# Four chunks of B and C in the state-space part, projected with tokens on partitions and turned by transposing transfers

## The chip, the cores and the metric

The kernel runs on one core of a Trainium2 chip, as one program. The time is device microseconds of one execution; below the median of the runs is given with their lowest and highest. Times inside an execution are microseconds from the start of its span, as the hardware profiler recorded them.

## What is computed

Two transformer blocks run one after the other on x of 256 tokens x 2048 features, in fp32: block 0 mixes with differential attention, block 1 with a state-space model (Mamba-2 style), and each is followed by a gated feed-forward network. The change lies in block 1's mixer:

```python
proj = h @ w_in                      # 256 x 2048 times 2048 x 10304
z, xbc, dt = jnp.split(proj, [4096, 4096 + 6144], axis=-1)
xbc = silu(causal_conv4(xbc, conv_w) + conv_b)       # along the tokens, each column for itself
xs, bm, cm = jnp.split(xbc, [4096, 4096 + 1024], axis=-1)
...
cb = jnp.einsum('btgn,bsgn->btsg', cc, bc)           # state products, 8 groups
y_intra = jnp.einsum('btsg,btsgh,bsghp->btghp', cb, decay, xdt)
...
return rms_norm((y + d_skip * xs) * silu(z)) @ w_out
```

B (bm) and C (cm) are columns 8192 to 10239 of the projection, x is columns 4096 to 8191, z columns 0 to 4095, and the last 64 columns are the step sizes dt. The convolution runs over time with four taps, so the kernel wants it with features on partitions and tokens along the free dimension, where a tap is a shifted slice.

## The kernel before, in words

Every weight matrix is streamed from DRAM in units of 256 rows x up to 512 columns. For a unit SyncE issues the load (`split_unit`, L261, a ring of 7 buffers named raw), ScalarE casts it to the rounded type fp32r (wh, L264), VectorE computes the remainder (wl = raw - wh), and TensorE makes three products per tile of 128 rows: wh with the high and the low part of the activations (ah, al), and wl with the high part. wh and wl have rings of 4 buffers: the cast of a unit waits until TensorE has ended the unit four before it. The remainder is put into VectorE's program one step late (`low_parts`, `lagging`), behind whatever the step before it issued there. Line 126 in the profile is a helper through which all of TensorE's and VectorE's instructions go, so tiles tell them apart: mm, wk and po are PSUM banks, bc holds B and C, xc the x columns of one group.

There are two ways to multiply a unit. `products` (through `push_k4`) makes the 128 tokens of a half the stationary operand and the weights the moving one: n columns per matmul, 2 x 2 x 3 matmuls per unit, tokens on partitions in the result. `feature_products` (through `push_features`) makes 128 weight columns stationary and the 256 tokens moving: n/128 x 2 x 3 matmuls of 256 columns per unit, features on partitions in the result.

The order of the work is written by generators. Each unit popped from the queue is one tick (`tick`), which steps every active generator once; a `yield` is a wait of one tick. The order of a chunk's follow-up work is thus fixed against the units of the chunks behind it, on all engines. Each of ScalarE, VectorE, TensorE and SyncE takes its instructions in that order. Beside the units run "ada" jobs (`dot_job`): SyncE loads 512 KB of the modulation matrix into the same ring raw (L498), and VectorE multiplies and sums it; in the stretch of B and C two per chunk.

Block 1 goes through its columns in the order 9856 (448 columns: 3 tiles of C and dt), 8192 (512), 8704, 9088, 9472 (384 each), then x0, z0, x1, z1, ... x7, z7 (512 each). All are eight units long.

- Chunk 9856 has tokens on partitions and is turned by TensorE (`conv_tokens`).
- Chunks 8192 to 9472 have features on partitions (`push_features`), and `conv_features` convolves them straight out of PSUM (`conv_tile`: one ScalarE instruction for the last tap and the bias, three VectorE instructions for the others), one tile of 128 features per tick, then a silu on ScalarE. x7 is done in the same way.
- Chunks x0 to x6 have tokens on partitions and go through `conv_turned` (L1856): ScalarE copies the two PSUM banks into the room of xc as 16-bit halves, all low halves ahead of all high ones; two ticks later SyncE issues two transposing transfers of 16-bit elements (L1864) into a room that is free by then (`y_turned`); three ticks later ScalarE puts the halves of two tiles together into the tile xin (L1870) and the convolution runs on that.

When the last chunk of B and C is convolved, `state_products` multiplies B with C for the eight groups, two groups per tick, and then loads the decay data of group 0 from DRAM by GpSimd's queue (`load_decay`, 1 MB). `y_steps` of group 0 uses that after z0.

Of the kernel before, what the change touches and what calls it, by code (L numbers as in the profile page):

```python
# [15 lines left out]
U16 = mybir.dt.uint16  # L16
# [80 lines left out]
def block_kernel(ctx: ExitStack, tc: tile.TileContext, x, x_t, columns_in, ssd_columns, da_columns, c, ada_w,  # L97
# [53 lines left out]
    def tmp(name="tmp"):  # L151
        return t2.tile([128, 512], F32, tag="t2", name=name)
# [1702 lines left out]

    def conv_turned(banks, xc, g):  # L1856
        hs = [xc[:, 2 * b:2 * b + 2, :].rearrange("p k t -> p (k t)").bitcast(U16) for b in range(2)]
        for b in range(2):
            act.copy(hs[b].rearrange("p (e f) -> p e f", e=2), banks[b].bitcast(U16).rearrange("p (f e) -> p e f", e=2))
        xT = [half_tiles(y_turned(g + 1)[:, b]) for b in range(2)]  # L1860
        for _ in range(2):
            yield
        for b in range(2):
            sp.dma_start_transpose(xT[b], hs[b])  # L1864
        for _ in range(3):
            yield
        for p in range(2):
            xin = tmp("xin").rearrange("p (k t) -> p k t", k=2)
            for b in range(2):
                act.copy(xin[:, :, b * 128:(b + 1) * 128].bitcast(U16).rearrange("p k (t e) -> p k t e", e=2),  # L1870
                         xT[b].rearrange("p (e k) t -> p k t e", e=2)[:, 2 * p:2 * p + 2])
            for i in range(2):
                conv_tile(xin[:, i, :], xc[:, 2 * p + i, :], 4 * g + 2 * p + i)
                yield
        act.activation(xc, xc, AF.Silu)
        yield

    def x_steps(g, banks):
        gp, h0 = S["gp"], 8 * g
        xc = gp.tile([128, 4, 256], F32, tag="xc", name="xc")  # L1880
        if g < TURNED:
            yield from conv_turned(banks, xc, g)
        else:
            yield from conv_features(banks, 4, xc, 4 * g)
# [126 lines left out]
    for col, n in ((9856, 448), (8192, 512), (8704, 384), (9088, 384), (9472, 384)):  # L2011
        bk = Banks()
        if n == 448:
            cross(end, norm, wi, col, n, bk, enter)
        else:
            norm.push(wi, col, n, bk, True)

        def take_bc(bk=bk, n=n, col=col):
            nt = 3 if n == 448 else n // 128
            t0 = (col - 8192) // 128  # L2020
            gens = [(conv_tokens if n == 448 else conv_features)(bk(), nt, S["bc"][:, t0:t0 + nt, :], 32 + t0)]
            if n == 448:
                gens.append(step_sizes(bk()))
            if col == 9472:
                last = gens[0]

                def then():
                    yield from last
                    yield from state_products()
                gens = [then()]  # L2030
# [131 lines left out]
```

## Time and profile before

| what | us |
|---|---|
| median of 3 runs (lowest to highest) | 2579.22 (2576.81 to 2579.29) |
| the profiled execution, its own time | 2578.1 |
| its span, first to last instruction | 2576.4 |
| TensorE busy in the span | 2551.2 (99%) |
| VectorE busy | 2110.8 (82%) |
| ScalarE busy | 1507.5 (59%) |
| stretch of chunks 8192 to 9472 (1213.34 to 1289.73), VectorE busy in it | 76.39, 62.88 |
| ScalarE busy in that stretch | 43.52 |

The page gives an engine's busy time and share of the span, then the chain of work that ended last by engine and line. A row of a timeline has start, duration, engine, line, operation, the tiles written and read, the shape, how many instructions were merged, and in brackets how long the engine had been idle and what ended the wait. A duration of a TensorE instruction reaches to the end of its pipeline, so the spacing of starts is its cost. A row of the stretches has the window, then the busy time of TensorE, its weight loads, VectorE, ScalarE and GpSimd with the number of instructions, the granted clock, the share of the DMA engines and GB/s. The clock was granted in full (0.999 on average).

### The profile page before, as it was taken

How to read it: one execution, taken by the hardware profiler on the slowest of the kernel's cores; microseconds unless marked ns; L12 is line 12 of the kernel's file. 1: busy time of each engine (PE TensorE's matmuls, PEld its weight loads, DVE VectorE, ACT ScalarE, POOL GpSimd, SP SyncE). 2: the span in 40 equal slices, each digit the busy share in tenths (PEclk: the TensorE clock that was granted, in tenths of full speed). 3: DMA queues.
4: the chain of work that ended last, by engine and by line, in shares of the span. 5: the costliest groups of instructions: out<-in, count | busy, mean ns of one | idle time of the engine just before them, and what ended most of it. 6: DMA issues, size and time to landing. Idle time of an engine off the chain costs nothing.

```text
span 2576.4 us, 34370 instructions
## 1 busy us (share of the span) xinstructions
PE 2551.2 (99%) x12144; PEld 2092.2 (81%) x12144; DVE 2110.8 (82%) x2955; ACT 1507.5 (59%) x2059; POOL 145.4 (6%) x225
## 2 busy tenths in 40 slices
PE   8999999999999999999999999999999999999999
PEld 5667778888888888888988888888888888888887
DVE  6779988778988898777878788888779999897675
ACT  4446654555655564446557777686566666665443
POOL 0014431000000000000000100000000000000000
PEclk9999999999999999999999999999999999999999
DMA  9987888699999869994677988878756667678884
GB/s 388 398 313 285 278 293 318 257 316 321 339 332 371 294 223 344 340 345 131 210 268 249 301 249 274 278 233 270 248 169 210 210 221 209 215 219 269 290 286 170
DMA packets 272989, 704.42 MB, mean 273 GB/s; under 512 B 101408, under 2 KB 109856, under 8 KB 271536
## 3 DMA queue, kind: packets, MB, share of 16 engines
q1 hardware_dynamic: 250960, 683.49, 76.8%
q10 hardware_dynamic: 17760, 4.43, 1.5%
q0 software_dynamic: 4096, 14.29, 1.5%
q8 instruction: 95, 1.56, 0.2%
q14 instruction: 78, 0.64, 0.1%
HBM read 680.53 MB, written 2.20 MB: 265 GB/s over the span
## 4 chain that ended last, share of the span: by engine, by line
PE 90%; DVE 4%; ACT 2%; DMA 2%; issue 1%; ACTq 0%; SPq 0%; POOL 0%; DVEq 0%; POOLq 0%
PE mm L126 62%; PE wk L126 22%; PE po L126 7%; DVE wl L126 1%; ACT wh L264 1%; DMA raw<-in_ssd_w_in 1%; DVE raw L126 1%; DMA raw<-in_ffn_w_gate_up 1%; DVE x L126 0%; DMA araw<-in_ada_w 0%; DMA raw<-in_da_w_in 0%; ACT hm L610 0%; ACTq L1991 0%; ACT e L1127 0%; DVE hm L126 0%
## 5 line engine op out<-in xcount | busy, mean ns | idle before, releaser
L264 ACT CAST wh<-raw 128x1024 fp32r<-128x1024 f32 (+3 forms) x822 | 842.2, 1037 | 744.0 <-PE mm L126 329.9
L126 DVE TENSOR_TENSOR wl<-raw,wh 128x1024 fp32r<-128x1024 f32 (+2 forms) x894 | 1043.5, 1184 | 208.8 <-ACT wh L264 207.6
L126 PE MATMUL mm<-wh,ah 128*128 128x512 f32 x2310 | 913.6, 395 | 3.1 <-ACT ah L988 1.7
L126 PE MATMUL mm<-wl,ah 128*128 128x512 f32 x2310 | 900.8, 390 | 3.0 <-DVE wl L126 3.0
L126 PE MATMUL mm<-wh,al 128*128 128x512 f32 x2310 | 901.7, 390 | 0.1
L126 PEld LDWEIGHTS mm<-wh,ah 128*128 128x128 f32 x2310 | 434.2, 188 | 108.9 <-issue 14.0
L126 PEld LDWEIGHTS mm<-wl,ah 128*128 128x128 f32 x2310 | 434.5, 188 | 96.1 <-DVE wl L126 8.5
L126 PEld LDWEIGHTS mm<-wh,al 128*128 128x128 f32 x2310 | 433.9, 188 | 94.4 <-DVE al L126 4.3
L126 DVE SCALAR_TENSOR_TENSOR raw<-raw,crow 128x1024 f32<-128x1024 f32 x320 | 389.9, 1220 | 0.0
L126 PE MATMUL wk<-wl,ah 128*128 128x512 f32 x594 | 231.8, 390 | 0.0
L126 PE MATMUL wk<-wh,al 128*128 128x512 f32 x594 | 231.3, 389 | 0.0
L126 PE MATMUL wk<-wh,ah 128*128 128x512 f32 x594 | 231.2, 389 | 0.0
L126 PEld LDWEIGHTS wk<-wl,ah 128*128 128x128 f32 x594 | 111.5, 188 | 25.5 <-DVE wl L126 2.6
L345 ACT CAST wh<-sums 128x1024 fp32r<-128x1024 f32 x72 | 75.6, 1050 | 93.8 <-PE mm L126 50.1
L126 PEld LDWEIGHTS wk<-wh,ah 128*128 128x128 f32 x594 | 111.5, 188 | 23.4
L126 PEld LDWEIGHTS wk<-wh,al 128*128 128x128 f32 x594 | 111.6, 188 | 22.8
L126 DVE TENSOR_TENSOR wl<-sums,wh 128x1024 fp32r<-128x1024 f32 x72 | 88.0, 1222 | 35.7 <-ACT wh L345 35.4
L552 POOL DMA_DIRECT2D gate_row<-grows x32 | 16.1, 511 | 1341.9 <-DVE grows L126 1341.9
L345 ACT CAST wh<-raw 128x1024 fp32r<-128x1024 f32 x72 | 59.0, 836 | 40.7 <-PE mm L126 25.0
L126 PE MATMUL po<-wh,ah 128*128 128x512 f32 x180 | 70.2, 390 | 0.0
L126 PE MATMUL po<-wh,al 128*128 128x512 f32 x180 | 70.0, 389 | 0.0
L126 PE MATMUL po<-wl,ah 128*128 128x512 f32 x180 | 70.0, 389 | 0.0
(371 smaller groups left out, 2582.9 us busy)
## 6 DMA issues: line engine op xcount, KB each, us to landing
raw<-in_ffn_w_gate_up SPq DMA_DIRECT2D x352, 512.0 KB, 4.8
raw<-in_ada_w SPq DMA_DIRECT2D x320, 512.0 KB, 5.3
raw<-in_ffn_w_down SPq DMA_DIRECT2D x176, 512.0 KB, 5.1
raw<-in_ssd_w_in SPq DMA_DIRECT2D x136, 512.0 KB, 5.7
raw<-in_da_w_in SPq DMA_DIRECT2D x90, 512.0 KB, 5.4
araw<-in_ada_w SPq DMA_DIRECT2D x64, 512.0 KB, 8.3
raw<-in_ssd_w_out SPq DMA_DIRECT2D x64, 512.0 KB, 5.0
raw<-in_da_w_out SPq DMA_DIRECT2D x32, 512.0 KB, 5.3
```

Of the source, the lines that this page charges most:

```text
L126: return fn(dst, *a, **k)
L264: act.copy(wh[:, at, :n], raw[:, at, :n])
L345: act.copy(wh[:, at, :], raw[:, at, :])
L552: pool.dma_start(gate_dram[hf][:, 32 * q:32 * q + 32], rows[o:o + 8, :])
```

## The change

Chunks 8192, 8704, 9088 and 9472 are now pushed with tokens on partitions, and `conv_turned` is generalized to n tiles, any destination and any room for the turned halves, and used for them. The room is that of y for groups 0, 2, 3 and 0. Between the last chunk's convolution and `state_products` one more tick is waited.

```diff
-    def conv_turned(banks, xc, g):
-        hs = [xc[:, 2 * b:2 * b + 2, :].rearrange("p k t -> p (k t)").bitcast(U16) for b in range(2)]
+    def conv_turned(banks, dst, n, cts, scratch):
+        flat = dst.rearrange("p k t -> p (k t)").bitcast(U16)
+        hs = [flat[:, b * 256 * n:(b + 1) * 256 * n] for b in range(2)]
         for b in range(2):
-            act.copy(hs[b].rearrange("p (e f) -> p e f", e=2), banks[b].bitcast(U16).rearrange("p (f e) -> p e f", e=2))
-        xT = [half_tiles(y_turned(g + 1)[:, b]) for b in range(2)]
+            act.copy(hs[b].rearrange("p (e f) -> p e f", e=2),
+                     banks[b][:, :n * 128].bitcast(U16).rearrange("p (f e) -> p e f", e=2))
+        turned = [half_tiles(scratch[:, b])[:, :2 * n, :] for b in range(2)]
         for _ in range(2):
             yield
         for b in range(2):
-            sp.dma_start_transpose(xT[b], hs[b])
+            sp.dma_start_transpose(turned[b], hs[b])
         for _ in range(3):
             yield
-        for p in range(2):
-            xin = tmp("xin").rearrange("p (k t) -> p k t", k=2)
+        for p in range(0, n, 2):
+            m = min(2, n - p)
+            xin = tmp("xin").rearrange("p (k t) -> p k t", k=2)[:, :m, :]
             for b in range(2):
                 act.copy(xin[:, :, b * 128:(b + 1) * 128].bitcast(U16).rearrange("p k (t e) -> p k t e", e=2),
...
-            norm.push(wi, col, n, bk, True)
+            norm.push(wi, col, n, bk)
...
-            gens = [(conv_tokens if n == 448 else conv_features)(bk(), nt, S["bc"][:, t0:t0 + nt, :], 32 + t0)]
+            dst = S["bc"][:, t0:t0 + nt, :]
+            if n == 448:
+                gens = [conv_tokens(bk(), nt, dst, 32 + t0)]
+            else:
+                gens = [conv_turned(bk(), dst, nt, 32 + t0, y_turned({8192: 0, 8704: 2, 9088: 3, 9472: 0}[col]))]
...
                     yield from last
+                    yield
                     yield from state_products()
```

On SyncE before, from the loads of chunk 8192 (width 1024, eight units) into those of the 384 chunks (L498 is a load for an ada job):

```order
L261 DMA raw<-in_ssd_w_in 128x1024 x8
L261 DMA raw<-in_ssd_w_in 128x2x384 x7
L498 DMA raw<-in_ada_w 128x1024
L261 DMA raw<-in_ssd_w_in 128x2x384 x4
L498 DMA raw<-in_ada_w 128x1024
L261 DMA raw<-in_ssd_w_in 128x2x384 x4
```

And now, in the same place (yT is the room of a group's y, by its number):

```order
L261 DMA raw<-in_ssd_w_in 128x1024 x8
L261 DMA raw<-in_ssd_w_in 128x2x384 x5
L1866 DMA_TRANSPOSE yT_11077<-bc 128x8x128 x2
L261 DMA raw<-in_ssd_w_in 128x2x384 x2
L498 DMA raw<-in_ada_w 128x1024
L261 DMA raw<-in_ssd_w_in 128x2x384 x4
L498 DMA raw<-in_ada_w 128x1024
L261 DMA raw<-in_ssd_w_in 128x2x384 x2
L1866 DMA_TRANSPOSE yT_11265<-bc 128x6x128 x2
```

A pair of transfers stands behind the load of the fifth unit of the next chunk, and the loads from its sixth unit on stand behind the pair; the same holds for all four pairs.

On VectorE before, the convolution of chunk 8704 while chunk 9088 is projected (three SCALAR_TENSOR_TENSOR on bc are one tile, wl is a unit's remainder, the one on raw is an ada job):

```order
L126 SCALAR_TENSOR_TENSOR bc<-mm,cw_4721,bc 128x253
L126 SCALAR_TENSOR_TENSOR bc<-mm,cw_4721,bc 128x254
L126 SCALAR_TENSOR_TENSOR bc<-mm,cw_4722,bc 128x255
L126 SCALAR_TENSOR_TENSOR bc<-mm,cw_4721,bc 128x253
L126 SCALAR_TENSOR_TENSOR bc<-mm,cw_4721,bc 128x254
L126 SCALAR_TENSOR_TENSOR bc<-mm,cw_4722,bc 128x255
L126 TENSOR_TENSOR wl<-raw,wh 128x2x384
L126 SCALAR_TENSOR_TENSOR raw,part_129<-raw,crow_99 128x1024
L126 SCALAR_TENSOR_TENSOR bc<-mm,cw_4721,bc 128x253
L126 SCALAR_TENSOR_TENSOR bc<-mm,cw_4721,bc 128x254
L126 SCALAR_TENSOR_TENSOR bc<-mm,cw_4722,bc 128x255
L126 TENSOR_TENSOR wl<-raw,wh 128x2x384 x4
```

And now the convolution of the same chunk, behind the remainders of 9088's units 5 to 7 (xin is the tile that ScalarE puts together from the turned halves):

```order
L126 TENSOR_TENSOR wl<-raw,wh 128x2x384 x3
L126 SCALAR_TENSOR_TENSOR bc<-xin,cw_4721,bc 128x253
L126 SCALAR_TENSOR_TENSOR bc<-xin,cw_4721,bc 128x254
L126 SCALAR_TENSOR_TENSOR bc<-xin,cw_4722,bc 128x255
L126 TENSOR_TENSOR wl<-raw,wh 128x2x384
L126 SCALAR_TENSOR_TENSOR raw,gate_cols<-raw,crow_98 128x1024
L126 SCALAR_TENSOR_TENSOR bc<-xin,cw_4721,bc 128x253
L126 SCALAR_TENSOR_TENSOR bc<-xin,cw_4721,bc 128x254
L126 SCALAR_TENSOR_TENSOR bc<-xin,cw_4722,bc 128x255
L126 TENSOR_TENSOR wl<-raw,wh 128x2x384
```

The convolution of a chunk moved from the head of the next chunk to its end: the remainder of the next chunk's eighth unit now stands behind the first tile, and those of the units after it behind the second and third. On TensorE the state products moved back by six units, from behind the third to sixth unit of x0 to behind the first to fourth of z0 (one to four units after x0's end).

More of the change, by code (lines that the diff above doesn't have):

```diff
@@ L1863, in conv_turned @@
         for b in range(2):
-            sp.dma_start_transpose(xT[b], hs[b])
+            sp.dma_start_transpose(turned[b], hs[b])
         for _ in range(3):
             yield
-        for p in range(2):
-            xin = tmp("xin").rearrange("p (k t) -> p k t", k=2)
+        for p in range(0, n, 2):
+            m = min(2, n - p)
+            xin = tmp("xin").rearrange("p (k t) -> p k t", k=2)[:, :m, :]
             for b in range(2):
                 act.copy(xin[:, :, b * 128:(b + 1) * 128].bitcast(U16).rearrange("p k (t e) -> p k t e", e=2),
-                         xT[b].rearrange("p (e k) t -> p k t e", e=2)[:, 2 * p:2 * p + 2])
-            for i in range(2):
-                conv_tile(xin[:, i, :], xc[:, 2 * p + i, :], 4 * g + 2 * p + i)
+                         turned[b].rearrange("p (e k) t -> p k t e", e=2)[:, p:p + m])
+            for i in range(m):
+                conv_tile(xin[:, i, :], dst[:, p + i, :], cts + p + i)
                 yield
-        act.activation(xc, xc, AF.Silu)
+        act.activation(dst, dst, AF.Silu)
         yield
@@ L1881, in x_steps @@
         if g < TURNED:
-            yield from conv_turned(banks, xc, g)
+            yield from conv_turned(banks, xc, 4, 4 * g, y_turned(g + 1))
         else:
```

## The prediction

> **What bounds the kernel now.** I read the page first (span, busy shares, and the line of the chain that ended last), then TensorE's timeline across the stretch that the change touches, then the stretches by chunk, then ScalarE's, VectorE's and SyncE's timelines around the transfers of 16-bit halves that this kernel already makes.
>
> ```profile
> span 2576.4 us, 34370 instructions
> PE 2551.2 (99%) x12144; PEld 2092.2 (81%) x12144; DVE 2110.8 (82%) x2955; ACT 1507.5 (59%) x2059; POOL 145.4 (6%) x225
> PE 90%; DVE 4%; ACT 2%; DMA 2%; issue 1%; ACTq 0%; SPq 0%; POOL 0%; DVEq 0%; POOLq 0%
> ...
> 1255.09:1272.41 17.32, 17.32 (x147) 17.32 (x146) 13.70 (x22) 8.60 (x13) 0.00 (x0) 1.00 0.77 254
> 1272.41:1289.73 17.32, 17.32 (x146) 17.32 (x145) 14.43 (x21) 9.22 (x13) 0.00 (x0) 1.00 0.78 262
> ```
>
> TensorE is the bound: 99% busy, 90% of the chain. The last two rows are the chunks of columns 9088 and 9472: 17.32 us each, TensorE without a gap, VectorE busy 13.70 and 14.43 us, ScalarE 8.60 and 9.22. So the change can gain only through cheaper matmuls, and lose only where TensorE must wait for its weights. I write U for TensorE's time on one unit (256 rows of weights) and n1, n2, ... for the units after a chunk's end; "te" is that end. Eight units are a chunk.
>
> **The change part by part.** *The matmuls.* TensorE's timeline, first and last rows of three unbroken series: 256 columns (130 groups of three), 448 columns (10 matmuls), 512 columns (111 matmuls).
>
> ```profile
> 1242.58 0.52 PE L126 MATMUL mm<-al,wh 128*128 128x256 f32 x3
> 1289.38 0.52 PE L126 MATMUL mm<-ah,wl 128*128 128x256 f32 x3
> ...
> 1211.12 0.36 PE L126 MATMUL mm<-wl,ah 128*128 128x448 f32 x1
> 1213.14 0.36 PE L126 MATMUL mm<-wh,al 128*128 128x448 f32 x1
> ...
> 1316.20 0.39 PE L126 MATMUL mm<-wh,ah 128*128 128x512 f32 x1
> 1341.36 0.39 PE L126 MATMUL mm<-wh,ah 128*128 128x512 f32 x1
> ```
>
> From start to start a matmul of 256 columns takes 46.80/390 = 0.120 us, of 448 columns 0.202, of 512 columns 25.16/111 = 0.2267. No row has 384: on the line from 256 to 512 it is 0.1734, by the step from 256 to 448 0.175, from 448 down by 64/192 of that step again about 0.175 (at most 0.177 by the step from 448 to 512). I take 0.174. Chunk 8192 goes from 192 x 0.120 = 23.04 to 96 x 0.2267 = 21.76 us (1.28 less), each 384 chunk from 144 x 0.120 = 17.28 to 96 x 0.174 = 16.70 (0.58 less; 0.3 to 0.6). Together 3.0 us less (2.2 to 3.1). U is 2.72 us in a 512 chunk, 2.09 in a 384 chunk.
>
> The Trainium skill (TensorE: Matmul & The Clock Gate, "Back-to-back issue gap") gives N/2.4 + 2.5 ns as the warm gap of a lone matmul, which would make the saving 0.6 us and the sum below 2.4 us dearer. The rows disagree: 120 and 227 ns where the rule has 109 and 216. The constant per matmul is some 13 ns here, so fewer matmuls are worth more.
>
> *The transfers.* Eight transposing transfers enter SyncE's queue, a pair per chunk, behind the load of n5 and ahead of n6, n7, one ada row block, n8. SyncE waits there until ScalarE has copied the chunk out of PSUM, and all loads from n6 on wait behind it. The x chunks already do this; their first (x0) has no work of state heads beside it. SyncE's timeline, x0's pair and x1's:
>
> ```profile
> 1308.77 0.33 SPq L498 DMA_DIRECT2D raw<-in_ada_w  x1
> 1319.11 3.42 SPq L1864 DMA_TRANSPOSE yT<-xc  x2
> 1322.62 1.50 SPq L261 DMA_DIRECT2D raw<-in_ssd_w_in  x3
> ...
> 1363.59 2.62 SPq L1864 DMA_TRANSPOSE yT<-xc  x2
> ```
>
> ScalarE after x0's end (the cast that TensorE's end releases, the two copies, the casts of n6 and n8, the copies and first convolution behind them), the same cast at x1's end, x1's cast of n8:
>
> ```profile
> 1317.13 1.06 ACT L264 CAST wh<-raw 128x1024 fp32r<-128x1024 f32 x1 [0.90 <-PE mm L126]
> 1318.08 1.92 ACT L1859 COPY xc<-mm 128x1024 uint16<-128x1024 uint16 x2
> ...
> 1326.10 1.05 ACT L264 CAST wh<-raw 128x1024 fp32r<-128x1024 f32 x1 [5.15 <-DMA raw<-in_ssd_w_in]
> ...
> 1329.62 1.05 ACT L264 CAST wh<-raw 128x1024 fp32r<-128x1024 f32 x1 [0.69 <-DVE raw L126]
> 1330.58 1.25 ACT L1870 COPY xin<-yT 128x512 uint16<-128x512 uint16 x2
> 1331.86 0.60 ACT L1739 ACTIVATE xc<-xin,cb,cw 128x256 f32<-128x256 f32 x1
> ...
> 1361.60 1.05 ACT L264 CAST wh<-raw 128x1024 fp32r<-128x1024 f32 x1 [1.67 <-PE mm L126]
> ...
> 1377.31 1.05 ACT L264 CAST wh<-raw 128x1024 fp32r<-128x1024 f32 x1 [1.91 <-DMA raw<-in_ssd_w_in]
> ```
>
> VectorE in the same place: its wait for n6's cast, the first convolution tile, then the low parts of n8, n9 and n10; and TensorE's first use of n10's low part:
>
> ```profile
> 1327.18 1.23 DVE L126 TENSOR_TENSOR wl<-raw,wh 128x1024 fp32r<-128x1024 f32 x1 [4.97 <-ACT wh L264]
> ...
> 1332.50 1.52 DVE L126 SCALAR_TENSOR_TENSOR xc<-xin,cw,xc 128x253 f32<-128x253 f32 x3 [1.81 <-ACT xc L1739]
> 1333.94 1.22 DVE L126 TENSOR_TENSOR wl<-raw,wh 128x1024 fp32r<-128x1024 f32 x1
> ...
> 1336.50 1.22 DVE L126 TENSOR_TENSOR wl<-raw,wh 128x1024 fp32r<-128x1024 f32 x1
> ...
> 1340.22 1.22 DVE L126 TENSOR_TENSOR wl<-raw,wh 128x1024 fp32r<-128x1024 f32 x1
> ...
> 1341.59 0.40 PE L126 MATMUL mm<-wl,ah 128*128 128x512 f32 x1
> ```
>
> n10's low part ends at 1341.44 and is used at 1341.59: at U = 2.72 the chain behind a pair has 0.15 us to spare. In a 384 chunk TensorE asks for n8 after 7 x 2.09 = 14.6 us instead of 19.0. The chain in that chunk, with these durations:
>
> ```profile
> L264 ACT CAST wh<-raw 128x768 fp32r<-128x768 f32 x24 | 19.5, 828 | 10.6 <-PE mm L126 10.6
> L126 DVE TENSOR_TENSOR wl<-raw,wh 128x768 fp32r<-128x768 f32 x24 | 22.0, 952 | 2.6 <-ACT wh L264 2.6
> ...
> 1251.33 1.22 DVE L126 SCALAR_TENSOR_TENSOR raw<-raw,crow 128x1024 f32<-128x1024 f32 x1
> ...
> 1252.47 2.69 DVE L126 TENSOR_TENSOR wl<-raw,wh 128x768 fp32r<-128x768 f32 x3
> ...
> 1325.00:1335.00 10.00, 10.00 (x45) 8.27 (x45) 5.94 (x8) 6.49 (x9) 0.00 (x0) 1.00 1.01 390
> ```
>
> - te to the first transfer: 1319.11 - 1317.13 = 1.98 us, less 0.22 (a cast of 768 for one of 1024) and 0.24 (a copy of 768, estimated at three quarters): 1.5; behind chunk 8192, whose copy is 1024 wide, 1.76.
> - The pair holds SyncE 2.6 us (x1; x0 3.4; for the narrower pairs down to an estimated 2.0).
> - To the landing of n8: at x0 1329.62 - 1322.53 = 7.1 us for three loads of 512 KB. Now it is the fourth, 384 + 384 + 512 + 384 KB, 128 KB more, 0.3 us at 390 GB/s: 7.4. Bounds: 3.6 (n6 at x0, 1326.10 - 1322.53, if all four land as soon as one did), and 11.1 at x1 (1377.31 - 1366.21), where n8 was the fourth too but decay data came between. I take 7.4, since x0 has the same queue without decay data.
> - n8's cast, two copies, convolution tile, three VectorE steps, low part: 1329.62 to 1335.16 = 5.5 us, less 0.22 and 0.27: 5.05.
>
> Sum 16.55 us behind a 384 chunk, 16.8 behind 8192. Then n9's low part waits for one ada product (1252.47 - 1251.33 = 1.14 us), a tile (1333.94 - 1332.50 = 1.44) and itself (0.87): 3.45 us, against U 2.09, another 1.36 late; n10's for a tile and itself, 2.31, another 0.2; 8192 has a fourth tile, 0.2 more.
>
> Losses: in chunk 8704, n8 late by 16.8 - 14.6 - 0.6 (small products of the step sizes that TensorE does there):
>
> ```profile
> 1237.02 0.56 PE L126 MATMUL wk<-dt,tri 128*128 128x64 f32 x4
> ...
> 1237.61 0.60 PE L126 MATMUL mm<-ah,wh 128*128 128x256 f32 x3
> ```
>
> that is 1.6; behind it n9 to n11, 1.8. Chunk 9088 so starts 1.8 late and its n8, wanted at 16.4, is late by only 0.15; then 1.6. Chunk 9472: wanted at 16.2, late by 0.35; then 1.6 at the start of x0. In x0 the units are longer and the chain (1.5 + 2.6 + 8.4 for four loads of 512 KB + 5.5 = 18.0) meets a demand at 1.6 + 19.0: covered. Total 7.1 us of new waits against 3.0 saved: **4.1 us slower**.
>
> *What costs nothing.* ScalarE's extra copies (two per chunk out of PSUM, four into the convolution's input; an estimated 4 us per 384 chunk by the rows above) fit, 13 of 16.7 us. VectorE's work is the same, 14.1 us of 16.7, but it leaves only 2.6 us for the waits that a pair forces on it (4.97 + 1.81 = 6.8 at x0). That is a second count of the same loss: (14.1 + 6.8 - 16.7) x 3 = 12.6 us at most. PSUM is freed earlier, no one waited for it. The state products move six units later, into z0 (1.22 us for two groups by the rows below); their cover for x0's units goes, and x0 has the 2.6 us shown above; z0 gains 4.9 us of TensorE work ahead of its own n8, more than the 2.7 us that the decay load (1024 KB at 390 GB/s) adds to its chain. That load, issued from GpSimd's queue, is wanted only after z0's end.
>
> ```profile
> 1304.71 1.47 PE L126 MATMUL wk<-bc 128*128 128x256 f32 x8
> 1305.93 0.48 PE L126 MATMUL mm<-wh,ah 128*128 128x512 f32 x1
> ```
>
> The sum: the profiled execution took 2578.1 us (span 2576.4), so 2578.1 + 4.1 = **2582.2 us**. The median of the three runs is 1.1 us above the profiled one, a difference that I leave in the range. A change of 0.2% (5.2 us) is about what a measurement of this kernel can tell from none; 4.1 us is 0.16%, inside it.
>
> **The rivals.** *The cover holds.* If the narrow pair and its loads come 1.95 us sooner (pair 2.0, n8 landing at 6.0), n8 is never late and what is left is n9's queue, little more than 1 us; with none of it the time is 2578.1 - 3.0 = 2575.1. For it: x0's chain just held. Against it: it held with 0.15 us at U = 2.72. The Trainium skill (DMA: Bandwidth & Descriptors, "Issuing engines are not separate DMA queues") calls the issuing time of a DMA usually small beside the DMA; a pair's 2.6 to 3.4 us, against 0.33 for a load, disagrees.
>
> *A late fourth load, slower than before.* If the pair takes 3.4 us as at x0 and n8 lands 8.4 us after it (x1's 11.1 less 2.7 for the decay load), each chain is 1.8 us longer: 7.1 + 3 x 1.8 = 12.5 us of waits, 2578.1 + 9.5 = 2587.6. It decides from 0.35 us per chain on (5.2 + 3.0 = 8.2 us of waits). For it: the 6.8 us that VectorE idles at x0.
>
> *The change does not pay on TensorE.* If a matmul of 384 columns takes the worst of the bounds (0.177), 0.9 us of the saving is gone: 2583.1. For it: 448 columns lie 2 ns above the line from 256 to 512. Against it: both neighbours are measured, and nothing lies between them but 3 ns. By the rule quoted above from the Trainium skill (TensorE: Matmul & The Clock Gate) it would be 2584.6; the rows of both neighbours speak against that.
>
> **How the numbers follow.** Waits as worked out, within 0.2%: 0.44. The late load: 0.33, all slower. The cover holds: 0.18, within 0.2%. The dearer matmul: 0.02, within. Faster by over 0.2% would need 5.2 us where the matmuls can give 3.1 and the stretch has no idle time to win back: 0.03. So faster 0.03, within 0.64, slower 0.33. The range, meant to hold the time 8 times in 10, runs from the cover case (2575) to the late load (2588); what is left out is an n8 later still.
>
> **What would show it.** Right: matmuls of 384 columns 0.174 us apart; eight more transposing transfers on SyncE; TensorE waiting for a low part (VectorE) near n8 and n9 of chunks 8704, 9088, 9472 and at x0's start, 7 us in all; ScalarE's cast of n8 waiting for a load. Wrong: those chunks at 16.7 us each with TensorE unbroken, or TensorE waiting anywhere else (state products, decay load, silu of x).

## The result, and the profile after

The changed kernel takes 2596.05 us (median of 6 runs, 2593.91 to 2598.75), the kernel before 2578.52 us (median of 6, 2576.81 to 2579.86). The ratio is 1.0069, 95% interval 1.0056 to 1.0082: 17.5 us slower, where 4.1 us had been forecast and 2588 was the end of the range. The forecast was wrong in size; the side and the place were right.

The page of the changed kernel, the same three lines as before:

```profile
span 2593.8 us, 33939 instructions
PE 2553.5 (98%) x11904; PEld 2085.7 (80%) x11904; DVE 2110.7 (81%) x2955; ACT 1524.2 (59%) x2083; POOL 145.1 (6%) x225
...
PE 86%; DVE 5%; DMA 4%; ACT 3%; issue 1%; SPq 0%; POOL 0%; ACTq 0%; DVEq 0%; POOLq 0%
```

The span grew by 17.4 us. TensorE is hardly busier (2553.5 against 2551.2, with its slow matmuls behind waits counted in), but its share of the chain fell from 90% to 86%, and VectorE's, the DMA's and ScalarE's rose. The group of TensorE's instructions between 1213 and 1390 us that waits, but for 0.2 us in another (columns: count, busy us and mean ns, then idle us just before them and what ended it):

```profile
L126 PE MATMUL mm<-wl,ah 128*128 128x512 f32 (+2 forms) x235 | 89.0, 379 | 13.6 <-DVE wl L126 13.6
```

Before, this stretch had no wait at all. TensorE's timeline there; the brackets hold the wait ahead of a matmul:

```profile
1253.91 0.69 PE L126 MATMUL mm<-wl,ah 128*128 128x384 f32 x1 [2.42 <-DVE wl L126]
1254.39 0.52 PE L126 MATMUL mm<-wh,al 128*128 128x384 f32 x1
1254.71 0.52 PE L126 MATMUL mm<-wh,ah 128*128 128x384 f32 x1
...
1275.84 0.44 PE L126 MATMUL mm<-wl,ah 128*128 128x384 f32 x1 [3.20 <-DVE wl L126]
...
1277.88 0.34 PE L126 MATMUL mm<-wh,ah 128*128 128x384 f32 x1
1279.29 0.44 PE L126 MATMUL mm<-wl,ah 128*128 128x384 f32 x1 [1.06 <-DVE wl L126]
...
1291.25 0.44 PE L126 MATMUL mm<-wl,ah 128*128 128x384 f32 x1 [0.55 <-DVE wl L126]
...
1291.88 0.33 PE L126 MATMUL mm<-wl,ah 128*128 128x384 f32 x1
...
1295.34 0.34 PE L126 MATMUL mm<-wh,ah 128*128 128x384 f32 x1
1298.52 0.69 PE L126 MATMUL mm<-wl,ah 128*128 128x384 f32 x1 [2.83 <-DVE wl L126]
...
1323.33 0.50 PE L126 MATMUL mm<-wl,ah 128*128 128x512 f32 x1 [1.71 <-DVE wl L126]
...
1327.04 0.50 PE L126 MATMUL mm<-wl,ah 128*128 128x512 f32 x1 [0.69 <-DVE wl L126]
```

From 1291.88 to 1295.34 lie 20 steps between matmuls of 384 columns, 0.173 us each: the saving of 3.0 us is there. The waits for low parts (wl) are at the end of chunk 8704 (2.4 us), of 9088 (3.2, and 1.1 in the next unit), of 9472 (2.8) and of x0 (1.7, and 0.7 in the next unit); x0's own pair brings two more, 0.5 and 0.7. They and two small ones add up to 13.9 us. Behind two of the long ones the matmuls start 0.32 us apart instead of 0.173 (1254.39 to 1254.71): there the granted clock is 0.50. That is 15 matmuls in all, 2.2 us. Worked back from the span, 17.4 + 3.0 = 20.4 us were lost: 13.9 of waits, 2.2 of half clock, and some 4 in the first matmuls behind waits and at chunk ends, which come 0.1 to 0.3 us late each.

One chain as it was predicted, behind the end of chunk 8704: SyncE, ScalarE and VectorE.

```profile
1259.11 2.57 SPq L1866 DMA_TRANSPOSE yT<-bc  x2
1261.77 1.21 SPq L261 DMA_DIRECT2D raw<-in_ssd_w_in  x2
1263.07 0.55 SPq L498 DMA_DIRECT2D raw<-in_ada_w  x1
1263.71 2.89 SPq L261 DMA_DIRECT2D raw<-in_ssd_w_in  x4
...
1283.05 2.57 SPq L1866 DMA_TRANSPOSE yT<-bc  x2
```

```profile
1257.55 0.84 ACT L264 CAST wh<-raw 128x768 fp32r<-128x768 f32 x1 [1.14 <-PE mm L126]
1258.29 1.49 ACT L1860 COPY bc<-mm 128x768 uint16<-128x768 uint16 x2
...
1270.73 0.84 ACT L264 CAST wh<-raw 128x768 fp32r<-128x768 f32 x1 [3.40 <-DMA raw<-in_ssd_w_in]
1271.47 1.26 ACT L1873 COPY xin<-yT 128x512 uint16<-128x512 uint16 x2
1272.76 0.60 ACT L1739 ACTIVATE bc<-xin,cb,cw 128x256 f32<-128x256 f32 x1
...
1280.76 0.85 ACT L1878 ACTIVATE bc<-bc 128x768 f32<-128x768 f32 x1 [3.40 <-DVE bc L126]
...
1282.23 1.50 ACT L1860 COPY bc<-mm 128x768 uint16<-128x768 uint16 x2
```

```profile
1266.35 1.96 DVE L126 TENSOR_TENSOR wl<-raw,wh 128x768 fp32r<-128x768 f32 x2 [1.17 <-ACT wh L264]
1273.40 1.52 DVE L126 SCALAR_TENSOR_TENSOR bc<-xin,cw,bc 128x253 f32<-128x253 f32 x3 [5.08 <-ACT bc L1739]
1274.84 0.95 DVE L126 TENSOR_TENSOR wl<-raw,wh 128x768 fp32r<-128x768 f32 x1
```

End of chunk to first transfer 1.56 us, the pair 2.57, to n8's cast 9.05, from there to the end of its low part 5.06: 18.2 us, against 14.6 wanted. The row to remember is VectorE's second one: the engine idles 5.08 us for the first convolution tile, while n8's cast was done at 1271.57. Its low part takes 0.95 us and could have been ready near 1272.5, when TensorE began to wait; but it stands behind the tile in VectorE's order and ends at 1275.79.

### The profile page after: what moved, and what is told of

It reads as the page before. It is cut to its first block, busy times and chain, and to the rows that moved or that the text cites. A ratio compares the mean times of both kernels' runs of the same rounds, so it can differ in the third digit from the quotient of the medians.

```text
span 2593.8 us, 33939 instructions
## 1 busy us (share of the span) xinstructions
PE 2553.5 (98%) x11904; PEld 2085.7 (80%) x11904; DVE 2110.7 (81%) x2955; ACT 1524.2 (59%) x2083; POOL 145.1 (6%) x225
## 4 chain that ended last, share of the span: by engine, by line
PE 86%; DVE 5%; DMA 4%; ACT 3%; issue 1%; SPq 0%; POOL 0%; ACTq 0%; DVEq 0%; POOLq 0%
PE mm L126 58%; PE wk L126 21%; PE po L126 6%; DVE wl L126 2%; DMA raw<-in_ssd_w_in 2%; ACT wh L264 1%; DVE raw L126 1%; DMA raw<-in_da_w_in 1%; DMA raw<-in_ffn_w_gate_up 1%; DVE bc L126 0%; ACT xin L1873 0%; DMA araw<-in_ada_w 0%; DVE x L126 0%; DMA raw<-in_ada_w 0%; DVE partoh L126 0%
## 5 line engine op out<-in xcount | busy, mean ns | idle before, releaser
L126 PE MATMUL mm<-wl,ah 128*128 128x512 f32 (+2 forms) x2438 | 948.0, 389 | 17.0 <-DVE wl L126 16.8
L126 PE MATMUL mm<-wh,ah 128*128 128x512 f32 (+2 forms) x2438 | 959.1, 393 | 3.6 <-ACT ah L988 1.7
L126 PE MATMUL mm<-wh,al 128*128 128x512 f32 (+2 forms) x2438 | 946.7, 388 | 0.1
L126 PEld LDWEIGHTS mm<-wl,ah 128*128 128x128 f32 x2438 | 459.0, 188 | 115.6 <-DVE wl L126 27.3
L126 PEld LDWEIGHTS mm<-wh,ah 128*128 128x128 f32 x2438 | 458.7, 188 | 111.0 <-issue 14.3
L126 PEld LDWEIGHTS mm<-wh,al 128*128 128x128 f32 x2438 | 458.6, 188 | 95.6 <-DVE al L126 4.3
```

Of the source, the lines that this page charges most:

```text
L126: return fn(dst, *a, **k)
```

## The experiments

The theory after the result: the lost time comes of one chain (copies, pair, late loads, copies into xin, convolution tile, low part), tied together by VectorE's order. Rivals: the transfers or the loads alone; a loop from a late tile through silu into the next pair; the extra tick ahead of the state products. Ratios are to the kernel before on the same chip. "Waits" are TensorE's between 1213 and 1390 us, from the rows of its groups. An interval of 0.1% to each side is 2.6 us, so a difference between two runs of the table is known to some 4 us.

| run | what differs from the changed kernel | ratio, 95% interval | waits, us |
|---|---|---|---|
| (changed kernel) | | 1.0069, 1.0056 to 1.0082 | 13.8 |
| late_silu | silu later | 1.0067, 1.0052 to 1.0082 | 13.4 |
| act_issue | pairs issued by ScalarE | 1.0101, 1.0082 to 1.0120 | 22.4 |
| no_tick | without the extra tick | 1.0058, 1.0043 to 1.0073 | 12.8 |
| no_ada | no ada jobs in the stretch (control: 1.0010, 1.0000 to 1.0019) | 1.0052, 1.0037 to 1.0067 | 10.1 |
| plain_dma | plain copies for the transfers | 1.0041, 1.0027 to 1.0055 | 8.5 |
| later3 | pairs three ticks later | 1.0032, 1.0021 to 1.0043 | 4.9 |
| one_pair | only 8192 turned | 1.0030, 1.0019 to 1.0042 | 6.1 |
| one_no_tick | the same, without the tick | 1.0028, 1.0017 to 1.0039 | 5.5 |
| no_taps | no VectorE steps in the convolution | 1.0026, 1.0017 to 1.0036 | 4.5 |
| conv2 | convolution two ticks later | 1.0020, 1.0011 to 1.0030 | 6.6 |
| idle_pairs | pairs that nobody reads | 1.0014, 1.0005 to 1.0024 | 3.0 |
| mm_only | no turning | 1.0007, 0.9997 to 1.0016 | 2.9 |
| later_three | pairs later, 9472 as before | 1.0002, 0.9993 to 1.0011 | 1.4 |
| te_turn | turned by TensorE, 9472 as before | 0.9996, 0.9987 to 1.0006 | 0 |
| mm_no_tick | no turning, no tick | 0.9990, 0.9981 to 0.9999 | 0.3 |

### The matmuls alone, with and without the tick

```diff
-                gens = [conv_turned(bk(), dst, nt, 32 + t0, y_turned(...))]
+                gens = [conv_slices(bk(), nt, dst, 32 + t0)]   # conv_tile on banks[k % 2][:, 0:256]
```

> The four chunks are projected with tokens on partitions, and the turning is left out: the convolution reads slices of PSUM at the head of the next chunk, as before the change (B and C so hold other numbers; the number and widths of the convolution's instructions are unchanged). Theory (matmuls are cheaper by 3.0 us, all the loss lies in the turning): 3 us under the kernel before, 2575 to 2576, TensorE unbroken from 1213 on, matmuls of 384 columns 0.173 apart. Rival (the wider projection itself brings waits, as its units are shorter and its weights are wanted sooner): 2578 or more, with TensorE waiting for wl in this stretch.

Measured 2580.94 us against 2578.16. TensorE ran through the four chunks with no more than two waits of 0.2 us, but waited 1.85 and 0.76 us in z0. GpSimd's and ScalarE's timelines there:

```profile
1320.09 0.59 POOL L1912 DMA_DIRECT2D abc<-acd  x1 [73.47 <-DVE cb L126]
```

```profile
1330.42 1.04 ACT L264 CAST wh<-raw 128x1024 fp32r<-128x1024 f32 x1 [10.35 <-DMA raw<-in_ssd_w_in]
```

The decay load (1 MB) went out 2.2 us behind x0's first transfer (1317.91), and the cast of n6 waited 10.35 us for its load. Neither expectation had this; the rival had the time, but with waits in another place. Only the tick, which moves the state products one unit back, could have put the decay load there, so it was taken out:

```diff
                     yield from last
-                    yield
                     yield from state_products()
```

> As the run that left the turning out (slices of PSUM convolved at the head of the next chunk), and the change's extra tick ahead of the state products is taken out too. With the tick, the decay load (1 MB, GpSimd) was issued 2.2 us behind x0's first transfer, and n6 to n8 landed 9.7 to 11.1 us after their issue instead of 3.4 to 5.8; without the change it is issued 1.9 us ahead of that pair. Theory (the tick moves the decay load into x0's pair, and that gives the 3 us back): the decay load is again ahead of the pair, TensorE unbroken near 1331, 2575 to 2576, ratio 0.9985 to 0.9992. Rival (the shorter stretch alone brings x0 its waits): 2578 to 2581 as with the tick.

```profile
1316.00 0.58 POOL L1912 DMA_DIRECT2D abc<-acd  x1 [69.58 <-PE mm L126]
```

```profile
1326.12 1.05 ACT L264 CAST wh<-raw 128x1024 fp32r<-128x1024 f32 x1 [6.36 <-DMA raw<-in_ssd_w_in]
```

The load is ahead of the pair again, the cast waits 4 us less, TensorE not at all in z0: 2577.78 against 2579.01 us. The tick alone is worth 1.0007 / 0.9990, about 4.4 us, where nothing is turned. The gain of the matmuls shows, though only just, 0.3 to 4.9 us by the interval. The time lies above what the theory gave (2575 to 2576), the ratio within it.

### Turning by TensorE

```diff
-            norm.push(wi, col, n, bk)
+            norm.push(wi, col, n, bk, col == 9472)
...
+            gens = [(conv_features if col == 9472 else conv_tokens)(bk(), nt, dst, 32 + t0)]
```

> Chunks 8192, 8704 and 9088 projected with tokens on partitions, but turned by TensorE at the head of the next chunk (20 transposes of 128x128, 0.09 us each, 1.8 us), 9472 as before the change, without the extra tick. Theory (tokens on partitions are no burden; the transfers and the late convolution behind them are): 2.4 us saved by the matmuls less 1.8, and no wait over 0.5 us: 2576 to 2579. Rival (any turning puts the convolution too late for VectorE): waits for wl of 3 us or more in the 384 chunks, 2581 or more.

2577.66 us, no wait in the stretch: the theory's case. Tokens on partitions are no burden when the turned tile is there at once. By the estimate the 20 transposes give back 1.8 of the 2.4 us that the matmuls save; the interval cannot tell the rest from nothing.

### One link of the chain at a time

```diff
-                conv_tile(xin[:, i, :], dst[:, p + i, :], cts + p + i)
+                conv_tile(xin[:, i, :], dst[:, p + i, :], cts + p + i, taps=0)
```

> The changed kernel without the three VectorE steps of each of the 13 convolution tiles of these chunks (ScalarE's first step and silu stay, so B and C lack three of four taps). It takes 1.44 us a tile off VectorE, 18.7 us in all, and leaves every load, transfer and copy in place. Theory (the chain to n8's low part is late as a whole, and the next low parts queue behind a tile each): n8's chain is 1.4 us shorter, n9's and n10's 2.9 and 4.3; waits fall from 13.9 us to 3 to 5, 2583 to 2587. Rival (VectorE has no lead left, 14 of 16.7 us a chunk, and that is all of it): waits under 1 us, 2576 to 2579. Rival (loads alone): waits of 10 us stay, 2591 or more.

2585.91 us, the theory's case; TensorE's two waiting groups, 1.3 + 3.2 us:

```profile
L126 PE MATMUL mm<-wh,ah 128*128 128x512 f32 (+1 forms) x251 | 95.0, 378 | 1.3 <-ACT wh L264 1.3
L126 PE MATMUL mm<-wl,ah 128*128 128x512 f32 (+2 forms) x251 | 94.2, 375 | 3.2 <-DVE wl L126 3.2
```

Part of what is left is now a wait for ScalarE's cast, that is, for the load itself.

```diff
-            call(lambda: ada.update(rate=SSD_RATES[0]))
+            call(lambda: ada.update(rate=0.0))
```

> The changed kernel without ada jobs from chunk 8704 to the start of x0 (they are done later, at the higher rate there). In the changed kernel n8 lands 8.4 to 9.0 us behind the pair, not 7.4, and the ada row ahead of it lands 2.0 to 3.2 us behind n7 where a unit of 384 takes 1.0. Theory (that row and the ada product ahead of n9's low part tip the chain over the 14.6 us that a chunk gives): n8 lands 6.0 us or less behind the pair, the low part of n8 ends by 13.8 us behind the chunk's end, TensorE's waits in the three 384 chunks fall from 10 us to under 3, 2583 to 2587 (x0, whose ada rows are back, keeps its waits). Rival (the chain is late by its transfers, copies and convolution, ada or not): waits of 7 us or more stay, 2591 to 2597.

> The kernel before with the same ada jobs put off: the control of the run beside it. If the jobs fit later without a wait, within 1 us of the kernel before; if they crowd the x chunks, several us slower, and the run beside it is to be read against this one.

2591.10 us, and 2580.30 for the control: 10.8 us between them where the changed kernel has 17.5. So ada jobs are worth about 7 us here, known to some 5. By its own time and by its waits of 10.1 us this is the rival's case: the chain is late with or without ada jobs. And n8 did not land 6.0 us behind the pair: it landed 6.9, 8.2 and 7.2 us behind it. The load that comes third behind a pair is slow whether it is an ada row or a unit of 384, so my reading that the ada row holds n8 up was wrong. What may explain the 7 us is one load less ahead of n8, and VectorE without the products; the run takes both away at once and does not part them.

```diff
-            sp.dma_start_transpose(turned[b], hs[b])
+            sp.dma_start(turned[b], hs[b].rearrange("p (j t) -> p j t", t=128))
```

> The changed kernel with the eight transposing transfers of B and C as plain copies of the same bytes at the same place (the halves so stay unturned and B and C hold other numbers). Theory (place: loads wait on SyncE for the copies, and the convolution stands at the chunk's end, whatever the transfer): SyncE is held 1.2 us a pair, not 2.6, n8 comes 1.5 to 3 us sooner, but 8 us of waits stay: 2586 to 2591. Rival (the transposing form itself, its 2.6 us and its small packets, is the cost): waits under 3 us, 2576 to 2580. Rival (the form is worth nothing): 2594 to 2597.

2588.78 us. SyncE's row of the second pair, and TensorE's group:

```profile
1255.74 1.21 SPq L1867 DMA_DIRECT2D yT<-bc  x2
```

```profile
L126 PE MATMUL mm<-wl,ah 128*128 128x512 f32 (+1 forms) x245 | 92.3, 377 | 8.5 <-DVE wl L126 8.5
```

The pair holds SyncE 1.21 us instead of 2.57, and 8.5 us of waits stay, as the theory said. 1.2 to 1.4 us a pair, some 5 in all, were worth about 7.

```diff
-            sp.dma_start_transpose(turned[b], hs[b])
+            act.dma_start_transpose(turned[b], hs[b])
```

> The changed kernel, but the four pairs of B and C are issued by ScalarE, where they stand behind the same copies, so that no load waits behind them on SyncE. Theory (loads held behind the pair are the root of the loss, 20 us): n8 of the next chunk lands 5 us sooner or more, TensorE's waits fall below 3 us, 2576 to 2580. Rival (the convolution's late place on VectorE and ScalarE is the root, whoever issues): waits for wl of 10 us or more stay, 2590 to 2597. A second rival: ScalarE itself is held by the transfers, 2.6 us a pair, and its casts come late: 2580 to 2590, with TensorE or VectorE waiting for a cast that had its load in time.

2603.94 us, worse than any expectation. In the first two chunks the waits were smaller than in the changed kernel (1.1 and 1.8 us against 2.4 and 4.3), in the last two far larger. ScalarE's queue and its copies behind the third pair:

```profile
1278.07 1.25 ACTq L1866 DMA_TRANSPOSE yT<-bc  x1
1279.36 1.79 ACTq L1866 DMA_TRANSPOSE yT<-bc  x1
...
1289.60 0.67 ACT L1873 COPY xin<-yT 128x512 uint16<-128x512 uint16 x1 [5.28 <-DMA yT<-bc]
1296.12 0.67 ACT L1873 COPY xin<-yT 128x512 uint16<-128x512 uint16 x1 [5.85 <-DMA yT<-bc]
```

From SyncE a transfer of the changed kernel lands 2.8 us after its start (3.2 for the first pair, 4.3 for the last transfer); here these two took 11.5 and 16.7, beside loads that nothing held back any more, and TensorE waited 10.5 us at once (and 8.2 us behind the fourth pair). The Trainium skill (DMA: Bandwidth & Descriptors, "Issuing engines are not separate DMA queues") says that DMAs run on the same 16 engines and interleave whoever issues them; the landings here fit that, and show what it can cost. By these landings the loads held back on SyncE are a loss, but holding them back also keeps the pair short.

### The order on VectorE

```diff
+        for k in range(n):                       # at the head of the next chunk, from PSUM slices
+            conv_tile(banks[k % 2][:, 0:256], dst[:, k, :], cts + k)
+            yield
+            if k == 1: ...                       # the pair, from a spare room, at its old place
```

> The four chunks with tokens on partitions; ScalarE copies the halves into a spare room and the eight transfers go out from SyncE at their place in the changed kernel, but nobody reads what they bring: the convolution takes slices of PSUM at the head of the next chunk (B and C so hold other numbers), without the extra tick. Theory (the chain must run through loads, copies, convolution step and VectorE's three steps to be late; without the last three it ends at 1.6 + 2.6 + 8.5 + 0.7 + 1.3 = 14.7 us behind a chunk's end, against 14.6 wanted): waits under 1 us a chunk, 2576 to 2580. Rival (loads held behind the pair are enough): waits for wl of 6 us or more in the 384 chunks, 2584 or more.

2581.82 us, between the two cases and nearer the theory: 3.0 us of waits (0.22 at n8 and 1.07 behind it in two chunks each, 0.23 in two others). Against the run without turning and without the tick (0.9990) the pairs, the copies ahead of them and the loads held behind them cost 0.24%, some 6 us; the changed kernel without the tick (1.0058, below) lies another 11 us higher. That larger part comes with the copies into xin and the convolution, which wait for the pair's data. So everything was left in, and only the copies into xin and the convolution moved:

```diff
-        for _ in range(3):
+        for _ in range(3 + lag):                 # lag=2 for B and C, and no extra tick
             yield
         for p in range(0, n, 2):
```

> The changed kernel (without the extra tick) with the pairs where they are, but the copies and the convolution behind them two ticks later, so that on VectorE the low parts of n8 and n9 stand ahead of the first tile. Theory (VectorE's order ties the low parts to the transfers: it waits 5 us for the tile while n8's cast is done): the waits at n8 fall from 2.4 to 3.2 us to 1 or less, those of the stretch from 13.9 us in all to 3 to 6, 2582 to 2587. Rival (the loads behind the pair are late by themselves): waits of 8 us or more, 2590 or more. What the later convolution pushes back at x0 and z0 may cost 1 to 5 us, as with the later pairs.

2584.20 us: 12.6 us less than the changed kernel by the ratios, and 9.8 us less than the changed kernel without the tick, from which it differs by `lag` alone. The theory's case, with 6.6 us of waits where it had 3 to 6. VectorE from n8's low part of chunk 9088 on:

```profile
1269.26 0.96 DVE L126 TENSOR_TENSOR wl<-raw,wh 128x768 fp32r<-128x768 f32 x1 [0.70 <-ACT wh L264]
...
1271.28 0.95 DVE L126 TENSOR_TENSOR wl<-raw,wh 128x768 fp32r<-128x768 f32 x1
1273.17 1.52 DVE L126 SCALAR_TENSOR_TENSOR bc<-xin,cw,bc 128x253 f32<-128x253 f32 x3 [0.93 <-ACT bc L1739]
```

The low parts of n8 (1269.26) and n9 (1271.28) are done before the tile, for which VectorE idles 0.93 us instead of 5.08. 3.7 us of waits are left up to the start of x0, and one of 2.9 behind it, at 1347. This is the most direct run: the same transfers, loads and arithmetic in another order on two engines. TensorE no longer waits at n8 of chunks 8704 and 9088, where it lost 2.4 and 3.2 us, although the two pairs ahead of them go out no earlier (1.4 and 3.9 us behind the first matmul of the next chunk, 1.4 and 1.8 in the changed kernel). On ScalarE n8's cast stands ahead of the copies into xin in both, so for n8 it is VectorE's order that differs. What remains above the run without turning, 0.30% or 8 us, is about what the pairs cost that nobody reads.

```diff
-        for _ in range(2):
+        for _ in range(2 + lag):                 # lag=3 for B and C: the pair, and all behind it
             yield
```

> The changed kernel with the four pairs three ticks later, so that the loads of n6 to n8 stand ahead of the pair on SyncE, and the copies are long done when SyncE comes to it; the convolution follows three units later, in the chunk after. Theory (what is late is the loads of n6 to n8, which wait on SyncE for ScalarE's copies and then for the pair): TensorE's waits fall to 3 us or less and the matmuls' 3.0 us show, 2575 to 2581. Rival (the loads behind the later pair are late by as much, only by other units, as the raw buffers are no deeper): 2588 to 2597. Second rival (it holds in the 384 chunks, but x0's own pair meets the decay load, as where the turning was left out, 5 us): 2581 to 2584.

2587.73 us: between the second rival and the first. The four chunks lost 1.3 us, as hoped, but the convolutions pushed into x0 delayed x0's own turned halves:

```profile
1347.48 1.12 PE L126 MATMUL wk<-ident,xc 128*128 128x128 f32 x4 [3.18 <-ACT xc L1878]
```

and behind 1390 TensorE waited another 4.5 us. With 9472 left as before:

> The pairs three ticks later, as before, for 8192, 8704 and 9088 alone; 9472 as before the change and without the extra tick, so that x0 and the state products find what they found before. With all four later, the 384 chunks lost only 1.3 us, but x0 waited 3.2 us for its own turned halves and x1 and x2 5 us more. Theory (the cost of the later pairs lay in the state products and x0 that they pushed back): waits of 1.3 to 2 us in the 384 chunks against 2.4 us saved, nothing behind: 2576 to 2580. Rival (a pair costs its 2 us or more wherever it stands): 2582 or more.

2580.54 us, no different from the kernel before, waits of 1.4 us: the theory's case, at the upper end of its time. Three pairs can be placed so that they cost no more than the matmuls save; 2.4 us is all there is to win, and this measurement does not show any of it.

### Loops, ticks and single pairs

```diff
+        for _ in range(lag):                     # lag=4 for 8192, 8704, 9088
+            yield
         act.activation(dst, dst, AF.Silu)
```

> The changed kernel, but the silu of the first three turned chunks is issued four ticks later, behind the next chunk's copies out of PSUM. Theory (the third and fourth pairs start 5.2 and 4.4 us behind their chunk's end because the copies stand behind a silu that waits for VectorE): these starts fall to about 1.6 us, the waits near 1295 and 1321 shrink from 4.5 us to below 1, 5 to 7 us in all: 2589 to 2591. Rival (VectorE's and the loads' lateness comes of the transfers on SyncE alone and only moves): the pairs start sooner but TensorE's waits stay within 2 us of the changed kernel's, 2594 to 2597.

2596.80 us: the rival. In the changed kernel the third pair starts 5.2 us behind its chunk's end (1277.88 to 1283.05), since the copies of 1282.23 stand behind the silu of 1280.76 that waits 3.40 us for VectorE. Moved, the silu and its table load came between n8's cast and the copies into xin, and VectorE waited there:

```profile
1274.98 1.52 DVE L126 SCALAR_TENSOR_TENSOR bc<-xin,cw,bc 128x253 f32<-128x253 f32 x3 [7.33 <-ACT bc L1739]
```

So this run took the loop out at one place and lengthened the chain at another: TensorE waited 5.5 us at that n8, and chunk 9088 now takes 24.1 us, where in the changed kernel 9472 took 24.0 and the others 20 to 21. One thing it does show: the fourth pair started 2.0 us behind its chunk's end instead of 4.4, and x0, which lost 2.4 us to it in the changed kernel, did not wait for n8 or n9 any more. That the third and fourth pairs start late is not the root of all: the first two did not, and TensorE waited 2.4 and 3.2 us behind them.

> The changed kernel without the extra tick ahead of the state products. With the turning left out that tick was worth 4 us, as it put the decay load into x0's pair; in the changed kernel the state products stand in z0, 18 us behind that pair. Theory (no part of the loss here): 2594 to 2597, the waits the same. Rival (it has one): 2592 or less, with the small waits of z0 near 1355 gone.

2593.24 us, between the cases, its interval overlapping the changed kernel's. Whether the tick has a part of 1 to 3 us in the changed kernel is open. TensorE's first three waits here, at n8 of chunk 8704, in the unit behind it, and at n8 of 9088:

```profile
1253.69 0.44 PE L126 MATMUL mm<-wl,ah 128*128 128x384 f32 x1 [2.15 <-DVE wl L126]
1257.13 0.45 PE L126 MATMUL mm<-wl,ah 128*128 128x384 f32 x1 [1.07 <-DVE wl L126]
1273.42 0.44 PE L126 MATMUL mm<-wl,ah 128*128 128x384 f32 x1 [1.01 <-DVE wl L126]
```

The clock stayed full behind the first, the second wait is new, and the third is 1.01 us instead of 3.20.

```diff
-            norm.push(wi, col, n, bk)
+            norm.push(wi, col, n, bk, col != 8192)   # and conv_features for the three others
```

> Only chunk 8192 is projected with tokens on partitions and turned; 8704, 9088 and 9472 stay as before the change. This prices one pair without a pair behind it. Theory (a late pair makes the next one later: silu of a chunk waits on ScalarE for VectorE's late last tile, ahead of the next chunk's copies): 1.3 us saved, one gap of 2.4 us near 1251, its pipeline and the half clock behind it 1.6, so about 2.7 us over the kernel before, 2581 to 2582. Rival (every pair costs alike, a quarter of the 17.5 us): 4.4 us over, 2583. The prediction's sum for this pair: 3.4 us of waits less 1.3, 2.1 us over.

> Only chunk 8192 turned, as in the run with one pair, without the extra tick. With the tick it was 8.4 us slower than the kernel before, and its x0 waited 1.3 us behind the decay load. Theory (about 4 us of that were the tick's): 2581 to 2583, the waits of 1.8 us near 1254 and 2.9 near 1266 to 1270 stay, those behind 1330 go; one pair then costs some 5 us with the 1.3 us saved, and four pairs, 20 us, cost about four times one. Rival (x0's waits are the first pair's late echo): 2585 to 2588.

2586.53 and 2585.51 us: 8 and 7 us slower, more than the theories gave, and the tick is not it: without it the waits of 1.3 us behind 1330 shrink to 0.5, but the ratio hardly moves. The second time is the rival's, though its echo in x0 was not there. TensorE's waiting group of the second run:

```profile
L126 PE MATMUL mm<-ah,wl 128*128 128x256 f32 x144 | 26.1, 291 | 5.0 <-DVE wl L126 5.0
```

1.9 and 1.0 us at the pair, 2.0 in the chunk behind it, which has no pair: VectorE, 18.1 of 19.2 us busy there (1253.3 to 1272.5), carries the delay on into the convolution at that chunk's head. One pair so costs more than a quarter of four.

## Why the prediction was wrong, step by step

- *Matmuls, 0.174 us and 3.0 us less.* Right: 0.173, and the run without turning shows the gain.
- *End of chunk to first transfer, 1.5 to 1.76.* Right for two pairs (1.8 and 1.6), wrong for the others (5.2 and 4.4), where a silu that waits for a late tile stands ahead of the copies. The prediction took ScalarE's queue at that point as empty.
- *The pair, 2.6 us.* Right, 2.57 to 2.65.
- *n8 lands 7.4 us behind it.* Mis-sized: 8.4, 9.0, 7.7 and 8.8 us, 1.1 more on average. The load that goes out third behind a pair is slow. And the x0 of before, from which the 7.4 came, was not quite without decay data: GpSimd issued the decay load at 1317.18, 1.9 us ahead of the pair.
- *From n8's cast to the end of its low part 5.05 us.* Right: 5.06.
- *The sum over the chunks: "Chunk 9088 so starts 1.8 late and its n8, wanted at 16.4 [...], is late by only 0.15", 0.35 for 9472, and x0 covered.* This is the step that failed: waits of 13.9 us stood in place of 7.1. It failed at two places.
  - The sum let the waits of n9 to n11, behind a chunk's end, put off the demand for the next n8. Behind the first pair n9's low part was as late as reckoned, 3.45 us behind n8's (1253.85 to 1257.30), but TensorE did not wait for it: at half clock the 11 matmuls in between took 3.4 us, against 2.0 in chunk 9088. So the delay fell ahead of the chunk's end, put off the next pair as well, and gave no slack; 9088 met a chain of 18.2 and paid 3.2 at n8 and 1.1 behind it. Where the clock stayed full, in the run without the tick, n9 waited 1.07 and 9088's n8 only 1.01: there this reasoning held.
  - Chunk 9472 paid 3.6, x0 paid 2.4 behind the fourth pair, and x0's own pair brought another 1.2, where the sum had 1.95 for 9472 and nothing for the rest. That is 5.2 of the 6.8 us of waits that were missing. The third and the fourth pair start late, behind the silu named above; x0's 2.4 us were gone when that silu was moved. For 9472 the runs do not part the late start from the rest.
- *The second count*, VectorE's slack of 2.6 us a chunk against 6.8 us of forced idling, gave 4.2 us a chunk, 12.6 in all, and was called an upper bound of the same loss. Chunks 8704, 9088 and 9472 took 4.4, 3.8 and 7.3 us longer than 16.7, slow matmuls and all: it was nearer than the chain, and no bound. In 9472 VectorE idled 8.7 us for late casts and tiles, not 6.8. That VectorE's order is behind it is what the later convolution shows (1.0020 for 1.0058).
- *Half clock behind waits* (2.2 us) and the slow first matmuls were put at nothing in the sum; they are about 6.5 of the 20.4 us lost, as much as the missing waits. With the waits alone the time would have been 2578.1 + 13.9 - 3.0 = 2589, one microsecond beyond the range.
- *State products and decay load, "wanted only after z0's end".* True of the data. But the load shares the DMA engines' time, and one tick can put it onto x0's pair: 4.4 us without the turning. In the changed kernel its part is open.
- *The rivals.* "A late fourth load" had the right sign, and its 12.5 us of waits are near the 13.9, in part by luck: n8 did land 8.4 us behind the pair, but the pair took 2.6 us and not 3.4, and neither x0's waits nor the half clock are in it. The cover did not hold.

## What to carry to other kernels

When a transfer is put between two steps of an in-order engine, look at what stands behind the waiting step on that engine: here a low part that was ready waited 3 us behind a tile that was not. Count such a chain anew for every chunk from that chunk's own end, ask what stands ahead of its first step on each engine, and when a count by the slack of the nearly full engine gives a larger loss than the chain, take the larger one seriously. Give the matmuls behind a wait a price of their own. And a tick that moves a large load is an edit of its own; time it apart.

## What the runs showed of the hardware that was not expected

The granted clock fell to half behind some short waits. Stretches of the changed kernel behind the waits of 2.4, 3.2 and 2.8 us (PEclk is the column behind POOL's), then one of the run without VectorE's steps:

```profile
1254.00:1257.00 3.00, 3.00 (x10) 3.00 (x11) 2.93 (x6) 2.37 (x4) 0.00 (x0) 0.50 0.47 131
...
1276.00:1280.00 4.00, 2.94 (x16) 2.62 (x17) 3.89 (x8) 1.34 (x2) 0.00 (x0) 1.00 0.36 98
...
1299.00:1302.00 3.00, 3.00 (x12) 2.85 (x11) 2.93 (x6) 1.62 (x3) 0.00 (x0) 0.60 0.54 176
```

```profile
1285.00:1289.00 4.00, 3.63 (x12) 3.63 (x13) 1.33 (x3) 1.43 (x3) 0.00 (x0) 0.59 1.00 378
```

It halved behind waits of 2.42 and 2.83 us, not behind 3.20, and in the other run behind waits of 1.08 and 0.55 us in close sequence. The Trainium skill (TensorE: Matmul & The Clock Gate, "What's actually happening") has the clock at half after at least one idle window of about 3.4 us, in a free-running grid of windows. The traces agree on the grid: in the changed kernel the clock is at half from 1253.62 to 1257.03 and from 1297.99 to 1301.40, 3.41 us each, and the two starts are 13 times 3.41 us apart. They do not agree that the window must be idle. TensorE's busy time in four windows of that grid (the third number of a line; the clock halved behind the first and the last window):

```profile
1250.20:1253.62 3.42, 1.28 (x8) 0.96 (x6) 2.08 (x4) 3.39 (x7) 0.00 (x0) 1.00 0.69 258
1270.68:1274.10 3.42, 1.97 (x12) 1.65 (x10) 0.67 (x2) 3.34 (x6) 0.00 (x0) 1.00 1.04 391
1274.10:1277.51 3.41, 1.67 (x9) 1.67 (x10) 3.34 (x7) 3.22 (x6) 0.00 (x0) 1.00 0.19 43
1294.58:1297.99 3.41, 1.10 (x7) 0.78 (x5) 1.85 (x4) 3.38 (x6) 0.00 (x0) 1.00 1.03 416
```

The wait of 3.20 us lies across a line of the grid, at 1274.10, and left each of its two windows about half busy. In fourteen of the traces, between 1225 and 1400 us, every window at full clock with up to 1.60 us busy was followed by half clock, and none with 1.82 us or more; from 1.67 to 1.79 both occur. So in these runs the clock halves behind a window that is busy for less than about half of its time, and whether a given wait makes one depends on where the grid happens to lie, which differs from run to run.

A transposing transfer of 128 x 6 x 128 halves holds SyncE's queue 1.23 to 1.28 us, a plain copy of the same bytes 0.6. The load that goes out third behind a pair lands 1.3 to 3.5 us behind the second, whatever it carries, where the second lands 1.0 to 1.9 behind the first; why was not found.
